# Linear attention on one core: K and V loaded with 8 KB from each row, KV products made by two halves of the array

## The chip, the cores and the metric

The kernel runs on one core of a Trainium2 chip. The metric is the device time of one execution in microseconds (us); lower is better.

## The reference

Q, K and V are float32 of shape 8 x 12 x 512 x 64: 96 heads of 512 rows with 64 columns.

```python
Q_feat = np.maximum(0, Q)
K_feat = np.maximum(0, K)
KV = np.einsum('bhkd,bhkv->bhdv', K_feat, V)
K_sum = np.sum(K_feat, axis=2)
numerator = np.einsum('bhqd,bhdv->bhqv', Q_feat, KV)
denominator = np.einsum('bhqd,bhd->bhq', Q_feat, K_sum)
return (numerator / (denominator[:, :, :, None] + 1e-10)).astype(np.float32)
```

There is no softmax: per head a 64 x 64 matrix KV and a vector of sums are made from K and V, and each row of Q is multiplied by them.

## The kernel before

The 96 heads are worked in twelve octets of eight heads (NO = 12), one octet in a step. An array X in DRAM is read as a flat row of numbers that is cut into blocks of 128 partitions (`view`).

**Loads.** Q of an octet is one block: each partition gets 8 KB of float32, which is 32 rows of a head, so a head lies on 16 partitions. K and V are cut into blocks of half an octet (g, four heads): each partition gets 4 KB, 16 rows, and a head lies on 32 partitions. For most octets (o < PAIRS = 9) the two blocks of K come in one transfer of two pieces of 4 KB for each partition (line 181), likewise V; the last three octets load each half by itself (line 187). These transfers are issued by POOL and turn float32 into bfloat16 on the way. Octet 0's K and V are loaded in float32 by SP in four transfers into two output buffers (line 277). POOL issues in the order K, V, Q of octets 1 to 7, and then a store of an octet before each further octet's loads; its transfers use ten semaphores in turn (LANES), so each issue waits until the transfer ten before it has landed. Stores of octets 0 to 3 go by POOL (line 262), the others by SP (line 265), where they wait for the first half of the last octet's K; the last octet's store is cut in two.

**The products of a step.** A matmul contracts over partitions, and four heads share the 128 partitions of a block, so heads are kept apart by masks of zeros. DVE's `prep_k` (line 201) writes K's positive part twice, in the columns s = 0 and 1, times `mask[:, 0, s]`, which keeps every second head. `prep_v` (lines 210 and 212, one of four by ACT) writes V twice, in t = 0 and 1, times `mask[:, 1, t]`. One matmul of 128 weight columns (two s by 64) and 132 moving columns (two t by 66) then yields four heads at once; the extra columns of ones give K_sum. Sixteen of them, one for each row of a partition, make up a half octet g, accumulated in `ps_kv[:, g]` (line 397); both halves' sums lie in one PSUM bank. `evac_kv` (line 227, four copies by ACT) brings the sums to `kvd`.

On PE a step is a loop body: transposes of q2 into ps_qt (line 390), the KV products (397), transposes of the octet before, ot, into ps_x (406), the denominators ps_den (384), and the numerators ps_x (384). DVE turns ps_den into reciprocals (`own`, `den`, `rec`, lines 240 to 247) and divides (`norm`, line 252) into the output buffer.

The order on each engine is written out by hand in `step`; the class `Order` adds the semaphore waits from what each operation reads and writes. PE's loop waits for named semaphores: q2, then a0 and d0 (masked K and V of the first half) and d1 (of the second), t0 and t1, qt and ev, n0 and n1. In `setup`, DVE writes the masks by memsets, prepares octet 0, and derives `mask_h`, which later picks each partition's own head out of the denominators, from a 128 x 128 identity that POOL makes. Two `prep_k` stand for each half octet, and `copy_q` (216) hands a landed Q to PE.

Of the kernel before, what the change touches and what calls it, by code (L numbers as in the profile page):

```python
# [89 lines left out]
def kernel(  # L90
# [8 lines left out]
    B, H, S, D = Q.shape  # L99
    assert D == 64  # L100
    P = 128
    D1 = D + 1
    D4 = D + 4
    NH = B * H
    R = S * 4 // P
    RQ = S * 8 // P
# [17 lines left out]
    def view(X, f):  # L124
        return X.rearrange("b h s d -> (b h s d)").rearrange("(n p f) -> n p f", p=P, f=f)

    Qr, Kr, Vr, Or = view(Q, RQ * D), view(K, R * D), view(V, R * D), view(out, RQ * D)

    ident = sb.tile([P, P], bf16, name="ident")
    ident32 = sb.tile([P, P], fp32, name="ident32")  # L130
# [13 lines left out]
    k_sb = [sb.tile([P, 2, R * D], bf16, name=f"k_sb{i}") for i in range(NI)]  # L144
    v_sb = [sb.tile([P, 2, R * D], bf16, name=f"v_sb{i}") for i in range(NI)]
    o_sb = [sb.tile([P, RQ, D], fp32, name=f"o_sb{i}") for i in range(NOUT)]
    ps_kv = psum.tile([P, 2, 256], fp32, name="ps_kv")
    ps_den = psum.tile([P, 2, 256], fp32, name="ps_den")
    ps_qt = [psum.tile([P, U // 2, P], bf16, name=f"ps_qt{j}") for j in range(2)]
    ps_x = [psum.tile([P, 1024], fp32, name=f"ps_x{j}") for j in range(2)]  # L150

    names = ["dve", "act", "pool", "pe", "q2", "a0", "d0", "d1", "qt", "ev", "t0", "t1", "n0", "n1"]
    lanes = {"pool": [f"gl{i}" for i in range(LANES)], "sp": [f"sl{i}" for i in range(4)],
             "last": [f"el{i}" for i in range(5)]}
    sems = {n: tc.alloc_semaphore("s_" + n) for n in names + sum(lanes.values(), [])}
# [2 lines left out]
    def lane(who):  # L158
        turn[who] += 1
        return lanes[who][(turn[who] - 1) % len(lanes[who])]  # L160
# [1 line left out]
    do = Order(nc, sems)  # L162

    def kv_src(g):
        if g < 2:
            kv = o_sb[g].rearrange("p (c r) d -> p c r d", c=2)
            return kv[:, 0], ("o", g, 0), kv[:, 1], ("o", g, 1)
        i, j = (g // 2) % NI, g % 2
        r = [x[i][:, j].rearrange("p (r d) -> p r d", d=D) for x in (k_sb, v_sb)]
        return r[0], ("k", i, j), r[1], ("v", i, j)  # L170

    def load_q(o):
        do.op("pool", lambda e: e.dma_start(out=q_sb[o % NI].rearrange("p u f -> p (u f)"), in_=Qr[o],  # L173
# [3 lines left out]
    def load_kv(o, halves=(0, 1)):  # L177
        i = o % NI
        if o < PAIRS:
            for n, X, t in (("K", Kr, k_sb), ("V", Vr, v_sb)):  # L180
                do.op("pool", lambda e: e.dma_start(out=t[i], in_=X[2 * o:2 * o + 2].rearrange("g p f -> p g f"),  # L181
                                                    single_packet=True),
                      writes=[(n.lower(), i, 0), (n.lower(), i, 1)], dma=lane("pool"))
            return
        for j in halves:
            for n, X, t in (("K", Kr, k_sb), ("V", Vr, v_sb)):
                do.op("pool", lambda e: e.dma_start(out=t[i][:, j], in_=X[2 * o + j], single_packet=True),  # L187
                      writes=[(n.lower(), i, j)], dma=lane("pool"))

    def load(o):  # L190
# [45 lines left out]
              reads=[("x", j)], writes=[("ot", j)], sem=f"t{j}")  # L236

    def denominators():
        ps = ps_den[:, 0].rearrange("p (u h c) -> p u (h c)", u=U, h=8)
        do.op("dve", lambda e: e.scalar_tensor_tensor(  # L240
            own.rearrange("p u h c -> p u (h c)"), ps, 1e-10,
            mask_h.rearrange("p h c -> p (h c)").unsqueeze(1).to_broadcast([P, U, 16]), op0=Alu.add, op1=Alu.mult),
            reads=["pd", "mask_h"], writes=["own"])
        do.op("dve", lambda e: e.tensor_reduce(  # L244
            out=den.rearrange("p (u c) -> p u c", c=2), in_=own.rearrange("p u h c -> p u c h"), op=Alu.add,
            axis=mybir.AxisListType.X), reads=["own"], writes=["den"])
        do.op("dve", lambda e: e.reciprocal(rec, den), reads=["den"], writes=["rec"])  # L247
# [17 lines left out]
            do.op("sp", lambda e: e.dma_start(out=to, in_=src), reads=keys, dma=lane("sp" if o < NO - 4 else "last"))  # L265

    KF = [[("kf", g, 0), ("kf", g, 1), ("vo", g, 0), ("vo", g, 1), ("vo1", g)] for g in range(2)]
    QT = [("qt", 0), ("qt", 1)]
    OT = [("ot", 0), ("ot", 1)]

    def memset(who, ap, value, key):
        do.op(who, lambda e: e.memset(ap, value), writes=[key] if isinstance(key, (str, tuple)) else key)

    def body():
        for g in range(2):
            for n, X, j in (("k", Kr, 0), ("v", Vr, 1)):
                do.op("sp", lambda e: e.dma_start(
                    out=o_sb[g].rearrange("p (c r) d -> p c (r d)", c=2)[:, j], in_=X[g]),
                    writes=[("o", g, j)], dma=lane("sp"))
        load_q(0)  # L280
        memset("pool", ident, 0.0, "ident")
        do.op("pool", lambda e: e.affine_select(out=ident, in_=ident, compare_op=Alu.not_equal, fill=1.0, base=0,
                                                pattern=[[-1, P]], channel_multiplier=1),
              reads=["ident"], writes=["ident"])
        for o in range(1, AHEAD + 1):
            load(o)
            if o == 1:
                setup()
        for o in range(NO + 1):
            step(o)  # L290
        nc.gpsimd.drain()
        for n in lanes["pool"] + lanes["sp"]:
            nc.gpsimd.wait_ge(sems[n], do.count[n])

    def setup():
        for h in range(4):
            for s in range(2):
                memset("dve", mask[32 * h:32 * h + 32, 0, s:s + 1], 1.0 if h % 2 == s else 0.0, ("m", h, s))
        for t in range(2):
            memset("dve", mask[:, 1, t:t + 1], 0.0, ("m", 4, t))  # L300
        for t in range(2):
            do.op("dve", lambda e: e.memset(mask[64 * t:64 * t + 64, 1, t:t + 1], 1.0), writes=[("m", 4, t), "mask"])
        for g in range(2):
            ones = vo[g][:, :, :, 1:D4 - 1]
            memset("dve", ones[:, :, :, 0:D + 2:D1], 0.0, ("vo1", g))
            for t in range(2):
                memset("dve", ones[64 * t:64 * t + 64, :, t, 0:D + 2:D1], 1.0, ("vo1", g))
        prep_k(0, 0)
        prep_k(0, 1)
        prep_v(0, 0, "dve", "d0")  # L310
        prep_v(0, 1, "act", "a0")
        do.op("dve", lambda e: e.tensor_copy(ident32, ident), reads=["ident"], writes=["ident32"])
        for c in range(2):
            do.op("dve", lambda e: e.tensor_reduce(
                out=mask_h[:, :, c], in_=ident32.rearrange("p (h b) -> p h b", h=8), op=Alu.add,
                axis=mybir.AxisListType.X), reads=["ident32"], writes=[("mh", c), "mask_h"])
        do.op("dve", lambda e: e.memset(kvf.bitcast(fp32)[:, 0:4 * D1], 0.0), writes=KVD, sem="n0")
        do.op("dve", lambda e: e.memset(kvf.bitcast(fp32)[:, 4 * D1:], 0.0), writes=KVD, sem="n1")
        copy_q(0)
        prep_k(1, 0)  # L320
        prep_k(1, 1)
        prep_v(1, 0, "dve")
        prep_v(1, 1, "dve", "d1")
        for j in range(2):
            nc.scalar.sem_inc(sems[f"t{j}"], 1)
            do.note("act", "act", (), (), f"t{j}", 1)

    def step(i):
# [15 lines left out]
        if not last:  # L344
            do.looped([("q2", r)], ["q2", "ident"], [("pq", 0)])
            do.looped([], ["q2", "ident"], [("pq", 1)])
            relu_q(0)
            relu_q(1)
            do.looped([("a0", r), ("d0", r)], KF[0], [("pk", 0)])
            do.looped([("d1", r)], KF[1], [("pk", 1)])  # L350
            evac_kv()
            if more and not late:
                prep_v(2 * i + 2, 1, "act", "a0")
                first()
# [25 lines left out]
    def products():  # L380
        pe = nc.tensor

        def mm(out_, lhsT, rhs):
            return pe.matmul(out_, lhsT, rhs, start=True, stop=True, skip_group_check=True)  # L384

        with pe.Fori(1, NO + 2, 1) as r:
            with pe.If(r < NO + 1):
                pe.wait_ge(sems["q2"], r)
                for u in range(U):
                    x = pe.transpose(ps_qt[u // 8][:, u % 8, :], q2[:, u, :], ident)  # L390
                    if u % 8 == 7:
                        x.then_inc(sems["pe"], 1)
                for g in range(2):
                    for s in ("a0", "d0") if g == 0 else ("d1",):
                        pe.wait_ge(sems[s], r)
                    for k in range(R):
                        x = pe.matmul(  # L397
                            ps_kv[:, g, 0:2 * (D + 2)].rearrange("p (t d) -> p t d", t=2),
                            kf[g][:, k, :, :].rearrange("p s d -> p (s d)"), vo[g][:, k, :, 1:D4 - 1],
                            start=(k == 0), stop=(k == R - 1), skip_group_check=True)  # L400
                    x.then_inc(sems["pe"], 1)
            with pe.If(r > 1):
                pe.wait_ge(sems["t0"], r)
# [6 lines left out]
            with pe.If(r < NO + 1):  # L410
                pe.wait_ge(sems["qt"], r)
                pe.wait_ge(sems["ev"], r)
                for u in range(U):
                    x = mm(ps_den[:, 0].rearrange("p (u h) -> p u h", u=U)[:, u], qt[:, u, :],
                           kvd[:, :, 0:2 * D1:2 * D1 - 1])
                x.then_inc(sems["pe"], 1)
                q = qt.rearrange("p u (h c) -> p u h c", h=8)
# [47 lines left out]
```

## Time and profile before

| what | before |
|---|---|
| median of 3 runs | 126.06 us (125.84 to 127.11) |
| the profiled execution | 125.83 us, of which the span is 124.1 |
| busy in the span | PE 87.2 us, DVE 87.5, ACT 78.4, POOL 29.6 |
| granted TensorE clock, mean | 0.903 |
| moved | 37.75 MB read from HBM, 12.58 MB written |

Times in the profile are microseconds from the start of the span. A row of the groups gives line, engine, operation, the tile written and the tiles read, shapes, the number of instructions, their busy time and mean duration in ns, and the idle time of the engine just before them with what ended it. PE is the matmuls, PEld the weight loads, which overlap them. A row of the timeline gives start, length, engine, line and operation; the square brackets hold the idle time before it and what ended that. In the page's slices each figure stands for a fortieth of the span, in tenths; PEclk is the granted clock of TensorE.

### The profile page before, as it was taken

To read this page: it belongs to the slowest core of one execution; us is meant where nothing else is said; L and a number is where in the kernel's file an instruction comes from. 1 tells how busy PE (TensorE), PEld (TensorE's weight loads), DVE (VectorE), ACT (ScalarE), POOL (GpSimd) and SP (SyncE) were. 2 spreads that over 40 slices of the span, in tenths; PEclk is the share of its full clock that TensorE was granted. 3 is DMA by queue.
4 is the path that set the end of the run, shared out by engine and by line. 5 is a ranking of instruction groups with operands and counts; after the bars stand their busy time and mean duration, and the time that the engine had idled before them with its cause. 6 is when DMAs were issued, how large, how long until landed. Compare 5 with 4: busy or idle time off the path is not lost.

```text
span 124.1 us, 2677 instructions
## 1 busy us (share of the span) xinstructions
PE 87.2 (70%) x1056; PEld 75.6 (61%) x1056; DVE 87.5 (71%) x180; ACT 78.4 (63%) x108; POOL 29.6 (24%) x50
## 2 busy tenths in 40 slices
PE   0007849755998989989796973998936996794600
PEld 0007739642995969879594961896923993592500
DVE  2746409369679999989979549799289319939530
ACT  0253299362949999999897980989953945953000
POOL 5992214122431442113111323151200000000000
PEclk9999995995589999999999997699995589999995
DMA  3999999999999999999999999999999999999993
GB/s 118 328 273 284 214 208 211 215 208 215 209 213 211 211 215 209 214 211 211 217 377 199 215 363 229 209 331 260 213 282 310 216 293 348 431 431 425 431 408 128
DMA packets 10260, 32.54 MB, mean 262 GB/s; under 512 B 912, under 2 KB 912, under 8 KB 8848
## 3 DMA queue, kind: packets, MB, share of 16 engines
q0 software_dynamic: 8384, 22.02, 83.1%
q1 hardware_dynamic: 1872, 10.49, 20.7%
q14 instruction: 4, 0.03, 0.1%
HBM read 37.75 MB, written 12.58 MB: 406 GB/s over the span
## 4 chain that ended last, share of the span: by engine, by line
DMA 66%; DVE 14%; PE 8%; issue 4%; POOL 3%; POOLq 0%; DVEq 0%; SPq 0%
DMA q_sb<-in_Q_dram 34%; DMA v_sb<-in_V_dram 20%; DMA k_sb<-in_K_dram 13%; DVE o_sb L252 8%; PE ps_kv L397 3%; PE ps_x L406 2%; DVE kf L201 2%; PE ps_qt L390 1%; DVE vo L212 1%; POOL q_sb L173 1%; POOL v_sb L181 1%; DVE ot_sb L235 1%; PE ps_x L384 1%; DVE den L244 1%; DVE rec L247 1%
## 5 line engine op out<-in xcount | busy, mean ns | idle before, releaser
L252 DVE TENSOR_TENSOR o_sb<-ps_x,rec 128x1024 f32<-128x1024 f32 x24 | 28.2, 1217 | 8.2 <-PE ps_x L406 7.9
L235 ACT COPY ot_sb<-ps_x 128x1024 f32<-128x1024 f32 x23 | 23.2, 1012 | 15.3 <-PE ps_x L384 13.8
L397 PE MATMUL ps_kv<-vo,kf 128*128 128x132 bf16 x384 | 28.9, 239 | 1.8 <-DVE vo L212 1.8
L397 PEld LDWEIGHTS ps_kv<-vo,kf 128*128 128x128 bf16 x384 | 26.9, 107 | 2.6 <-DVE vo L212 2.3
L384 PE MATMUL ps_x<-qt,kvd 128*128 128x256 bf16 x96 | 17.5, 316 | 13.5 <-DVE o_sb L252 13.1
L219 ACT ACTIVATE qt<-ps_qt 128x1024 bf16<-128x1024 bf16 x24 | 23.3, 1029 | 3.3 <-PE ps_qt L390 3.3
L227 ACT CAST kvd<-ps_kv 64x260 bf16<-64x260 f32 x48 | 18.0, 374 | 10.9 <-PE ps_kv L397 9.6
L390 PE MATMUL ps_qt<-ident,q 128*128 128x128 bf16 x192 | 16.6, 255 | 11.2 <-DVE q L216 11.2
L406 PE MATMUL ps_x<-ident,ot_sb 128*128 128x128 f32 x192 | 23.0, 273 | 1.7 <-DVE ot_sb L235 1.7
L390 PEld LDWEIGHTS ps_qt<-ident,q 128*128 128x128 bf16 x192 | 14.6, 117 | 13.7 <-DVE q L216 11.8
L406 PEld LDWEIGHTS ps_x<-ident,ot_sb 128*128 128x128 f32 x192 | 20.8, 141 | 2.0 <-issue 2.0
L216 DVE COPY q<-q_sb 128x2048 bf16<-128x2048 bf16 x12 | 8.2, 687 | 17.1 <-DMA q_sb<-in_Q_dram 16.1
L384 PEld LDWEIGHTS ps_x<-qt,kvd 128*128 128x128 bf16 x96 | 8.5, 108 | 19.0 <-DVE o_sb L252 17.7
L201 DVE TENSOR_SCALAR kf<-k_sb,mask 128x1024 bf16<-128x1024 bf16 x44 | 19.5, 467 | 0.6 <-PE ps_kv L397 0.6
L212 DVE TENSOR_SCALAR vo<-v_sb,mask 128x1024 bf16<-128x1024 bf16 x33 | 14.9, 481 | 0.0
L210 ACT ACTIVATE vo<-v_sb,mask 128x1024 bf16<-128x1024 bf16 x11 | 12.7, 1153 | 0.3
L173 POOL DMA_DIRECT2D q_sb<-in_Q_dram x12 | 7.5, 623 | 14.7 <-DMA v_sb<-in_V_dram 8.1
L384 PEld LDWEIGHTS ps_den<-kvd,qt 128*128 128x128 bf16 x192 | 6.0, 96 | 4.2 <-issue 4.2
L181 POOL DMA_DIRECT2D v_sb<-in_V_dram x8 | 5.8, 727 | 10.1 <-DMA k_sb<-in_K_dram 8.3
L384 PE MATMUL ps_den<-kvd,qt 128*128 128x16 bf16 x192 | 6.9, 179 | 1.8 <-ACT kvd L227 1.8
L181 POOL DMA_DIRECT2D k_sb<-in_K_dram x8 | 6.0, 751 | 7.5 <-DMA q_sb<-in_Q_dram 6.3
L187 POOL DMA_DIRECT2D k_sb<-in_K_dram x6 | 3.3, 544 | 11.7 <-DMA out_dram<-o_sb 4.2
(23 smaller groups left out, 32.8 us busy)
## 6 DMA issues: line engine op xcount, KB each, us to landing
out_dram<-o_sb SPq DMA_DIRECT2D x7, 1024.0 KB, 12.4
q_sb<-in_Q_dram POOLq DMA_DIRECT2D x12, 512.0 KB, 23.2
k_sb<-in_K_dram POOLq DMA_DIRECT2D x8, 512.0 KB, 24.6
v_sb<-in_V_dram POOLq DMA_DIRECT2D x8, 512.0 KB, 24.6
out_dram<-o_sb POOLq DMA_DIRECT2D x4, 1024.0 KB, 22.2
k_sb<-in_K_dram POOLq DMA_DIRECT2D x6, 256.0 KB, 17.9
v_sb<-in_V_dram POOLq DMA_DIRECT2D x6, 256.0 KB, 18.4
o_sb<-in_K_dram SPq DMA_DIRECT2D x2, 512.0 KB, 5.7
```

Source lines behind the costliest of these rows:

```text
L181: do.op("pool", lambda e: e.dma_start(out=t[i], in_=X[2 * o:2 * o + 2].rearrange("g p f -> p g f"), single_packet=True), writes=[(n.lower( ...
L201: do.op("dve", lambda e: e.tensor_scalar(kf[g % 2][:, :, s, :], src, scalar1=0.0, scalar2=mask[:, 0, s:s + 1], op0=Alu.max, op1=Alu.mult), ...
L210: make = lambda e: e.activation(to, src, Act.Copy, scale=m)
L212: make = lambda e: e.tensor_scalar(to, src, scalar1=m, scalar2=None, op0=Alu.mult)
L219: do.op("act", lambda e: e.activation(qt[:, j * (U // 2):(j + 1) * (U // 2)], ps_qt[j], Act.Relu), reads=[("pq", j)], writes=[("qt", j)], ...
L227: do.op("act", lambda e: e.copy(kvd[64 * c:64 * c + 64, s:8:2, c * D1:c * D1 + D1].rearrange("p (g t) d -> p g t d", t=2), ps_kv[64 * s:64 ...
L235: do.op(who, lambda e: e.copy(to, src) if who == "act" else e.tensor_copy(to, src), reads=[("x", j)], writes=[("ot", j)], sem=f"t{j}")
L252: do.op("dve", lambda e: e.tensor_tensor(o_sb[i][:, rs], ps_x[j].rearrange("p (r d) -> p r d", d=D), rec[:, rs].unsqueeze(2).to_broadcast( ...
L384: return pe.matmul(out_, lhsT, rhs, start=True, stop=True, skip_group_check=True)
L390: x = pe.transpose(ps_qt[u // 8][:, u % 8, :], q2[:, u, :], ident)
L397: x = pe.matmul(ps_kv[:, g, 0:2 * (D + 2)].rearrange("p (t d) -> p t d", t=2), kf[g][:, k, :, :].rearrange("p s d -> p (s d)"), vo[g][:, k ...
L406: x = pe.transpose(ps_x[u // 8][:, u % 8 * P:u % 8 * P + P], ot[:, u].rearrange("p h c -> p (h c)"), ident32)
```

## The change

K and V are cut as Q is: 8 KB for each partition, 32 rows of a head, a head on 16 partitions, eight heads on the 128. The transfers of a whole octet have one piece of 8 KB for each partition; those of half an octet (octet 0 and the last three) now take half of each 8 KB. So g is no longer four of the heads, but half of the rows of all eight.

The two masks together keep one head of four, which now leaves two of the eight. So each KV matmul is made twice, on partitions 0 to 63 and on 64 to 127, as matmuls of 64 rows by 128 columns. Each half of the array has its own sums in its own PSUM bank, over both g: 32 matmuls for each half where there were 16 for each g, so 64 in a step in place of 32. `ps_kv` takes two banks, and `ps_den` moves into the upper part of its second one. Therefore PE waits, ahead of the KV products, for a new semaphore dn, which `own` raises after reading ps_den. `mask[:, 0]` changes every 16 partitions and is computed from mask_h, which moves ahead of octet 0's preparation with ident32; the `vo` columns of ones are set by four memsets of 32 partitions in place of two of 64.

```diff
-    Qr, Kr, Vr, Or = view(Q, RQ * D), view(K, R * D), view(V, R * D), view(out, RQ * D)
+    Qr, Kr, Vr, Or = [view(X, RQ * D) for X in (Q, K, V, out)]
...
-    ps_kv = psum.tile([P, 2, 256], fp32, name="ps_kv")
-    ps_den = psum.tile([P, 2, 256], fp32, name="ps_den")
+    ps_kv = psum.tile([P, 2, 512], fp32, name="ps_kv")
+    ps_den = ps_kv[:, 1, 256:512]
...
-                do.op("pool", lambda e: e.dma_start(out=t[i], in_=X[2 * o:2 * o + 2].rearrange("g p f -> p g f"),
+                do.op("pool", lambda e: e.dma_start(out=t[i].rearrange("p j f -> p (j f)"), in_=X[o],
...
-                do.op("pool", lambda e: e.dma_start(out=t[i][:, j], in_=X[2 * o + j], single_packet=True),
+                do.op("pool", lambda e: e.dma_start(out=t[i][:, j], in_=X[o][:, R * D * j:R * D * (j + 1)],
+                                                    single_packet=True),
...
-            reads=["pd", "mask_h"], writes=["own"])
+            reads=["pd", "mask_h"], writes=["own"], sem="dn")
...
         for h in range(4):
-            for s in range(2):
-                memset("dve", mask[32 * h:32 * h + 32, 0, s:s + 1], 1.0 if h % 2 == s else 0.0, ("m", h, s))
-        for t in range(2):
-            memset("dve", mask[:, 1, t:t + 1], 0.0, ("m", 4, t))
-        for t in range(2):
-            do.op("dve", lambda e: e.memset(mask[64 * t:64 * t + 64, 1, t:t + 1], 1.0), writes=[("m", 4, t), "mask"])
+            for t in range(2):
+                do.op("dve", lambda e: e.memset(mask[32 * h:32 * h + 32, 1, t:t + 1], 1.0 if h % 2 == t else 0.0),
+                      writes=[("m", h, t), "mask"])
         for g in range(2):
             ones = vo[g][:, :, :, 1:D4 - 1]
             memset("dve", ones[:, :, :, 0:D + 2:D1], 0.0, ("vo1", g))
-            for t in range(2):
-                memset("dve", ones[64 * t:64 * t + 64, :, t, 0:D + 2:D1], 1.0, ("vo1", g))
+            for h in range(4):
+                memset("dve", ones[32 * h:32 * h + 32, :, h % 2, 0:D + 2:D1], 1.0, ("vo1", g))
+        do.op("dve", lambda e: e.tensor_copy(ident32, ident), reads=["ident"], writes=["ident32"],
+              sem="dn")
+        for c in range(2):
...
+        do.op("dve", lambda e: e.tensor_reduce(
+            out=mask[:, 0, :], in_=mask_h[:, :, 0].rearrange("p (a s) -> p s a", s=2), op=Alu.add,
+            axis=mybir.AxisListType.X), reads=["mask_h"], writes=["mask"])
         prep_k(0, 0)
...
-                    for s in ("a0", "d0") if g == 0 else ("d1",):
+                    for s in ("dn", "a0", "d0") if g == 0 else ("d1",):
                         pe.wait_ge(sems[s], r)
                     for k in range(R):
-                        x = pe.matmul(
-                            ps_kv[:, g, 0:2 * (D + 2)].rearrange("p (t d) -> p t d", t=2),
-                            kf[g][:, k, :, :].rearrange("p s d -> p (s d)"), vo[g][:, k, :, 1:D4 - 1],
-                            start=(k == 0), stop=(k == R - 1), skip_group_check=True)
+                        for h in range(2):
+                            ps = slice(64 * h, 64 * h + 64)
+                            x = pe.matmul(
+                                ps_kv[:, h, 0:2 * (D + 2)].rearrange("p (t d) -> p t d", t=2),
+                                kf[g][ps, k, :, :].rearrange("p s d -> p (s d)"), vo[g][ps, k, :, 1:D4 - 1],
+                                start=(g + k == 0), stop=(g == 1 and k == R - 1), skip_group_check=True)
```

More of the change, by code (lines that the diff above doesn't have):

```diff
@@ L146 @@
     o_sb = [sb.tile([P, RQ, D], fp32, name=f"o_sb{i}") for i in range(NOUT)]
-    ps_kv = psum.tile([P, 2, 256], fp32, name="ps_kv")
-    ps_den = psum.tile([P, 2, 256], fp32, name="ps_den")
+    ps_kv = psum.tile([P, 2, 512], fp32, name="ps_kv")
+    ps_den = ps_kv[:, 1, 256:512]
     ps_qt = [psum.tile([P, U // 2, P], bf16, name=f"ps_qt{j}") for j in range(2)]
     ps_x = [psum.tile([P, 1024], fp32, name=f"ps_x{j}") for j in range(2)]
-    names = ["dve", "act", "pool", "pe", "q2", "a0", "d0", "d1", "qt", "ev", "t0", "t1", "n0", "n1"]
+    names = ["dve", "act", "pool", "pe", "q2", "a0", "d0", "d1", "dn", "qt", "ev", "t0", "t1", "n0", "n1"]
     lanes = {"pool": [f"gl{i}" for i in range(LANES)], "sp": [f"sl{i}" for i in range(4)],
@@ L164, in kv_src @@
     def kv_src(g):
[L165 to L170, printed above, removed]
+        o, j = g // 2, g % 2
+        kv = (o_sb[0], o_sb[1]) if o == 0 else [x[o % NI].rearrange("p j (r d) -> p (j r) d", d=D) for x in (k_sb, v_sb)]
+        key = [("o", c, j) if o == 0 else (c, o % NI, j) for c in ((0, 1) if o == 0 else "kv")]
+        return kv[0][:, R * j:R * j + R], key[0], kv[1][:, R * j:R * j + R], key[1]
     def load_q(o):
@@ L238, in denominators @@
     def denominators():
-        ps = ps_den[:, 0].rearrange("p (u h c) -> p u (h c)", u=U, h=8)
+        ps = ps_den.rearrange("p (u h c) -> p u (h c)", u=U, h=8)
         do.op("dve", lambda e: e.scalar_tensor_tensor(
@@ L267 @@
     KF = [[("kf", g, 0), ("kf", g, 1), ("vo", g, 0), ("vo", g, 1), ("vo1", g)] for g in range(2)]
+    PK = [("pk", 0), ("pk", 1)]
     QT = [("qt", 0), ("qt", 1)]
@@ L274, in body @@
     def body():
-        for g in range(2):
-            for n, X, j in (("k", Kr, 0), ("v", Vr, 1)):
+        for j in range(2):
+            for c, X in enumerate((Kr, Vr)):
                 do.op("sp", lambda e: e.dma_start(
-                    out=o_sb[g].rearrange("p (c r) d -> p c (r d)", c=2)[:, j], in_=X[g]),
-                    writes=[("o", g, j)], dma=lane("sp"))
+                    out=o_sb[c][:, R * j:R * j + R].rearrange("p r d -> p (r d)"),
+                    in_=X[0][:, R * D * j:R * D * (j + 1)]), writes=[("o", c, j)], dma=lane("sp"))
         load_q(0)
@@ L305, in setup @@
             memset("dve", ones[:, :, :, 0:D + 2:D1], 0.0, ("vo1", g))
-            for t in range(2):
-                memset("dve", ones[64 * t:64 * t + 64, :, t, 0:D + 2:D1], 1.0, ("vo1", g))
+            for h in range(4):
[4 more added lines that the diff above has]
+            do.op("dve", lambda e: e.tensor_reduce(
+                out=mask_h[:, :, c], in_=ident32.rearrange("p (h b) -> p h b", h=8), op=Alu.add,
+                axis=mybir.AxisListType.X), reads=["ident32"], writes=[("mh", c), "mask_h"])
+        do.op("dve", lambda e: e.tensor_reduce(
+            out=mask[:, 0, :], in_=mask_h[:, :, 0].rearrange("p (a s) -> p s a", s=2), op=Alu.add,
+            axis=mybir.AxisListType.X), reads=["mask_h"], writes=["mask"])
         prep_k(0, 0)
@@ L311, in setup @@
         prep_v(0, 1, "act", "a0")
[L312 to L316, printed above, removed]
         do.op("dve", lambda e: e.memset(kvf.bitcast(fp32)[:, 0:4 * D1], 0.0), writes=KVD, sem="n0")
@@ L348, in step @@
             relu_q(1)
-            do.looped([("a0", r), ("d0", r)], KF[0], [("pk", 0)])
-            do.looped([("d1", r)], KF[1], [("pk", 1)])
+            do.looped([("dn", r), ("a0", r), ("d0", r)], KF[0], PK + ["pd"])
+            do.looped([("d1", r)], KF[1], PK + ["pd"])
             evac_kv()
@@ L413, in products @@
                 for u in range(U):
-                    x = mm(ps_den[:, 0].rearrange("p (u h) -> p u h", u=U)[:, u], qt[:, u, :],
+                    x = mm(ps_den.rearrange("p (u h) -> p u h", u=U)[:, u], qt[:, u, :],
                            kvd[:, :, 0:2 * D1:2 * D1 - 1])
```

## The prediction

> **What bounds the kernel now.** The page's slices come first, then its DMA queues: is anything busy from end to end?
>
> ```profile
> PEclk9999995995589999999999997699995589999995
> DMA  3999999999999999999999999999999999999993
> GB/s 118 328 273 284 214 208 211 215 208 215 209 213 211 211 215 209 214 211 211 217 377 199 215 363 229 209 331 260 213 282 310 216 293 348 431 431 425 431 408 128
> ...
> q0 software_dynamic: 8384, 22.02, 83.1%
> q1 hardware_dynamic: 1872, 10.49, 20.7%
> ```
>
> The DMA row is full in 38 of 40 slices. GB/s counts bytes written: a load that turns f32 into bf16 reads twice what it writes, so 211 in the middle is about 422 read, close to the 431 of the plain f32 stores at the end. The two queues together hold 103.8% of sixteen engines' span: packets overlap a little on an engine, so a packet's duration is not its cost. The spacing of transfers is. I read it from POOL's timeline, where each issue waits until the transfer ten before it has landed:
>
> ```profile
> 21.05 0.71 POOL L181 DMA_DIRECT2D v_sb<-in_V_dram  x1 [1.77 <-DMA k_sb<-in_K_dram]
> 23.49 0.56 POOL L173 DMA_DIRECT2D q_sb<-in_Q_dram  x1 [1.73 <-DMA v_sb<-in_V_dram]
> 25.94 0.70 POOL L181 DMA_DIRECT2D k_sb<-in_K_dram  x1 [1.90 <-DMA q_sb<-in_Q_dram]
> 28.49 0.71 POOL L181 DMA_DIRECT2D v_sb<-in_V_dram  x1 [1.85 <-DMA k_sb<-in_K_dram]
> 30.96 0.56 POOL L173 DMA_DIRECT2D q_sb<-in_Q_dram  x1 [1.75 <-DMA v_sb<-in_V_dram]
> ```
>
> An issue released by a K landing and the next one, released by V, differ by V's transfer: 2.44 us; then Q 2.45, K 2.55, V 2.47. A step of the loop takes three such transfers, 7.4 us. How much of that does the compute need? The timeline of one step in the middle:
>
> ```profile
> 61.73 2.06 PE L397 MATMUL ps_kv<-vo,kf 128*128 128x132 bf16 x32
> ...
> 63.08 0.69 DVE L216 COPY q<-q_sb 128x2048 bf16<-128x2048 bf16 x1 [0.62 <-DMA q_sb<-in_Q_dram]
> ...
> 63.62 1.91 PE L406 MATMUL ps_x<-ident,ot_sb 128*128 128x128 f32 x16
> ...
> 65.28 2.34 DVE L252 TENSOR_TENSOR o_sb<-ps_x,rec 128x1024 f32<-128x1024 f32 x2
> ```
>
> DVE is idle 0.62 us, waiting for Q's landing, so it needs about 6.8 of the 7.4 us. PE's loop is as long: from the division at 65.28 (2.34) over the ps_x products (0.61), the transposes (1.06), the KV products (2.06) to the first half of the L406 transposes (0.95), the blocks' recorded ends overlapping a little, the next division could start at about 72.05, 6.77 us later. Loads pace the steps; compute follows with some 0.65 us to spare. Last, the chain of what ended last, its end:
>
> ```profile
> 73.28 17.10 DMA q_sb<-in_Q_dram
> ...
> 97.82 3.00 PE ps_kv L397 x32
> ...
> 108.63 1.12 PE ps_kv L397 x16
> ...
> 116.52 2.36 DVE o_sb L252 x2
> ```
>
> The last wait on a load ends at 90.38; then 28.5 us of compute lead to 118.88, where the last half store can start. In the trace's landing records the last stores land every 2.45 us, the two halves at 121.7 and 122.95: they leave the queue without a gap. An unhindered half-MB transfer takes about 3.2 us (the first SP load, issued at 0.95, landed at 4.17), so the compute would allow an end at 122.1. The end is set by the transfers, and compute has about 0.8 us to spare there.
>
> **The change, part by part.**
>
> *K and V rows of 8 KB.* Sixteen transfers (K and V of octets 1 to 8) now have 128 packets instead of 256; octet 0 and octets 9 to 11 are still moved as 4 KB from each row. Q already has the new shape: 8 KB read, 4 KB written. So Q against K/V prices the edit. By durations (packet records of the trace): 173.7 ns for a K/V packet, 324.5 for a Q packet; 2 x 173.7 - 324.5 = 22.9 ns, times 2,048 pairs, over 16 engines: 2.9 us saved. That is the upper end, since durations overlap. By spacing: eighteen issue intervals from 18.57 to 63.28 average 2.51 us for K/V and 2.43 for Q; without one disturbed neighbouring pair (2.82 and 2.31), 2.48 and 2.45. Times 16: 1.3 or 0.5 us. A fit of packet starts over the steady stretch (155 ns for a K/V packet, about 303 for a Q packet) gives 7 ns x 2,048 / 16 = 0.9. The lower end is nothing. I take 0.7 us, between the spacings, which are nearest to what the queue does. As the transfers run to the end without a gap, 0.7 us earlier at octet 8 is 0.7 us earlier at the last store, and the last Q that compute waits for lands that much earlier too.
>
> *KV products by halves.* Each step's 32 pairs of weight load and matmul become 64 pairs of 64 rows, alternating between the halves, in two PSUM banks. No row of before shows matmuls of two halves side by side. The bounds:
>
> ```profile
> L397 PE MATMUL ps_kv<-vo,kf 128*128 128x132 bf16 x384 | 28.9, 239 | 1.8 <-DVE vo L212 1.8
> L397 PEld LDWEIGHTS ps_kv<-vo,kf 128*128 128x128 bf16 x384 | 26.9, 107 | 2.6 <-DVE vo L212 2.3 <-ACT vo L210 0.3
> ...
> L384 PE MATMUL ps_den<-kvd,qt 128*128 128x16 bf16 x192 | 6.9, 179 | 1.8 <-ACT kvd L227 1.8
> ```
>
> In the middle 32 pairs take 2.06 us, 64 ns each. One after another, 64 pairs take 4.1 us: +2.06 a step. If halves overlap wholly, what is left is issue: the ps_den block runs 16 pairs with only 16 moving columns in 0.58 us, 36 ns a pair, so 64 take 2.3 us: +0.25. A gain below 2.06 is excluded, since every pair still has a 128-column weight load and must be issued. I take +0.4, near the overlapping end, because the halves share neither rows nor PSUM bank. That is 7.2 us of PE loop against 7.4 us of loads, so it hides in the middle. Without the cover it would be 0.4 us times the steps. In the tail two KV blocks are on the path; of the second only the half after d1 is. That is 1.5 x 0.4 = 0.6 us, inside the 0.8 us to spare.
>
> On this the Trainium skill speaks both ways. "TensorEngine Tiling (Array Packing)", section "Key Properties", says that different tiles can execute weight loads and matmuls in parallel, which is the overlapping end; it also says that changing the tiling mode drains the engine, and each step changes it twice. "TensorE: Matmul & The Clock Gate", section "Single matmul latency", gives (398 + N)/2.4 ns warm; as an estimate two such drains at N = 132 are 0.44 us a step, by which the tail would grow by about 0.7 us more and the forecast rise to about 126.
>
> *ps_den in the second KV bank.* PE must now wait (dn) until own of the step before has read the denominators, ahead of its first KV matmul; queued behind are that block and all PE work after it. At 60.11 to 60.52 own is over before the KV block begins at 61.73, behind the ps_x products and transposes; in the tail own ends at 104.4 and KV begins at 107.1. Cost nothing; without the 1.06 us of transposes as cover, some 0.3 us a step. ACT's four ps_kv copies keep their form (64x260, 374 ns).
>
> *Setup.* The eight mask memsets and four more ones memsets are chained, at about 0.17 us wait each (as the vo memsets show); ident32, the two mask_h reductions (0.29 each) and a third now precede the first kf. Some 1 + 1 + 2 us later: the first kf goes from 4.20 to about 7.4, the first q copy from 9.35 to about 10.1. V's second half, landing at 12.7, then releases DVE as before; step 1's copy waits 4.15 us for Q in any case. PE would begin step 1 at most 0.3 us later, and it idles 0.76 us there. Cost nothing; uncovered, 0.3 us once. POOL and SP have as many issues in the same order.
>
> The sum against the profiled execution (125.83 us: span 124.1, 1.7 around it) is -0.7, 125.1; against the median of 126.06 it is **125.4 us**.
>
> **Rivals.**
>
> *The halves run one after another* (the change doesn't do what it says for PE). The KV block takes 4.1 us, the PE loop 6.77 + 2.06 = 8.83, more than the loads' 7.4, so PE becomes the pace. Step 1 starts at 18.3; nine steps on is 97.8 instead of 90.5. The tail grows from 28.5 to about 30 us (the KV blocks cost 0.9 and 1.4 more, the transposes, no longer after an idle stretch at the half clock of slices 30 and 31, 0.85 less). 127.8 and 3.2 us of store give 131 against 122.95: about 134 us. For it: consecutive weight loads of L397 are already 60 ns apart. Against: separate rows and banks. It decides from about +1.1 us a block: then the tail's 1.5 x 1.1 uses up the 0.8 to spare and the 0.7 gained; at +1.3, step 10 starts 0.8 us late and the end is near 128.
>
> *Packet durations are the cost.* Then all 2.9 us are gained in transfers: 123.2, if the compute tail, starting as much earlier, is at most 0.8 longer. Against: 103.8%, and Q's landings hardly closer than K's.
>
> *The rows don't matter at all*: 2.48 against 2.45 is chance, and PE stays hidden: 126.0, no change.
>
> **How the numbers follow.** Forecast 0.49 (own range 124.6 to 126.2); rows without effect 0.17; packet durations, wholly or half, 0.14; halves mostly or wholly serial 0.20, of which half lies above 129. Faster by over 1% (below 124.8, about what a measurement can tell here) are the third case and a little of the first: 0.20. Slower by over 1% is the serial case and some of its border: 0.24. The rest, 0.56, is within 1%. Range 123.9 to 129.0: one in ten above it, less than one in ten below.
>
> **What would show it.** Right: PE ps_kv blocks of 2.2 to 2.6 us in the middle, DVE's q copy still released by Q's landing each step, K/V issue intervals of 2.44 to 2.46, about 2,048 packets fewer in q0, a DMA row full to the end. Wrong: KV blocks near 4 us with DVE's division waiting for L406 in each step; intervals near 2.3 (durations were the cost) or unchanged; gaps between the last stores' landings, which would mean that the tail's compute sets the end.

## The result and the profile after

The changed kernel takes 130.33 us (median of 4, 130.05 to 134.69; the 134.69 ran at a mean granted clock of 0.71 and is not in the ratio). The kernel before took 126.05 beside it. The ratio is 1.0315 (95% interval 1.0242 to 1.0388); a second measurement on another chip gave 130.09 and 1.0342 (1.0309 to 1.0375). The forecast was 125.4 us with a range of 123.9 to 129.0. It was wrong in size and in sign.

The profiled execution has a span of 128.5 us, 4.4 more than before. First the groups, where the serial rival had placed the danger:

```profile
L400 PE MATMUL ps_kv<-vo,kf 64*128 64x132 bf16 x768 | 27.5, 230 | 2.1 <-DVE vo L211 2.1
...
L400 PEld LDWEIGHTS ps_kv<-vo,kf 64*128 64x128 bf16 x768 | 24.9, 100 | 4.0 <-DVE vo L211 2.3
```

There are twice as many matmuls, 768, and their busy time is 27.5 us, where 384 took 28.9. In the block the two halves overlap wholly. One step of the timeline shows it with its neighbours:

```profile
42.28 1.06 PE L391 MATMUL ps_qt<-ident,q 128*128 128x128 bf16 x16
...
43.28 2.07 PE L400 MATMUL ps_kv<-vo,kf 64*128 64x132 bf16 x64
...
45.27 1.97 PE L409 MATMUL ps_x<-ident,ot_sb 128*128 128x128 f32 x16
...
46.40 1.22 DVE L251 TENSOR_TENSOR o_sb<-ps_x,rec 128x1024 f32<-128x1024 f32 x1 [0.29 <-PE ps_x L409]
```

64 pairs take 2.07 us; 32 took 2.06. PE lost nothing in the block, so the transfers come next. The page's slices and queues:

```profile
DMA  3999999999999999999999999999999999999753
GB/s 94 233 269 273 249 214 214 214 213 212 214 213 214 212 214 213 213 217 212 282 307 209 258 322 152 223 339 232 206 328 251 209 338 422 415 423 416 321 237 138
...
q0 software_dynamic: 6336, 22.02, 78.8%
q1 hardware_dynamic: 1872, 10.49, 20.8%
q14 instruction: 4, 0.03, 0.1%
q8 instruction: 1, 0.02, 0.0%
```

The 2,048 packets are gone from q0, and the middle runs at 212 to 217. But slices 1 to 3, counted from 0, moved 233, 269 and 273 where they moved 328, 273 and 284, and the last three 321, 237 and 138 where they moved 431, 408 and 128. The end is no longer full: the DMA row falls to 7, 5, 3. And a row is new: one packet in a queue q8 of instructions. POOL's timeline shows where the transfers fall behind (each issue follows the landing of the transfer ten before it, named in the bracket):

```profile
23.66 0.69 POOL L179 DMA_DIRECT2D v_sb<-in_V_dram  x1 [2.77 <-DMA k_sb<-in_K_dram]
25.80 0.53 POOL L171 DMA_DIRECT2D q_sb<-in_Q_dram  x1 [1.46 <-DMA v_sb<-in_V_dram]
...
77.55 0.53 POOL L185 DMA_DIRECT2D k_sb<-in_K_dram  x1 [1.88 <-DMA out_dram<-o_sb]
80.47 0.53 POOL L185 DMA_DIRECT2D v_sb<-in_V_dram  x1 [2.40 <-DMA k_sb<-in_K_dram]
```

In the first pair K of octet 2 releases V's issue at 23.66; before, the same issue (K of octet 2 landed) came at 21.05. In the last pair the landing of octet 9's first half of K, half the size of a whole transfer, came 2.92 us after the store's; before, the same interval was 77.04 - 75.98 = 1.06:

```profile
75.98 0.53 POOL L187 DMA_DIRECT2D k_sb<-in_K_dram  x1 [2.08 <-DMA out_dram<-o_sb]
77.04 0.53 POOL L187 DMA_DIRECT2D v_sb<-in_V_dram  x1 [0.53 <-DMA k_sb<-in_K_dram]
```

A transfer is over when the last of its sixteen engines is. The landing records give all sixteen, so the distance from the first engine to the last is a measure of how far some engines are behind:

| first to last engine, us | Q of octet 2 | first K half of octet 9 | store of octet 10 |
|---|---|---|---|
| before | 0.49 | 0.80 | 1.11 |
| after | 1.85 | 3.58 | 4.08 |

From Q of octet 2 to the last load of a whole octet, landings 28 to 75 us after the start, this distance stays between 1.8 and 1.9 us: what is behind does not catch up. The records do not name the engines, so that it is the same one each time is inferred. At the store of octet 9 the first engine is done at 117.78, 0.9 us later than before (116.87), the last at 122.40, 4.4 later (117.99). From there the last engine's landings follow each other about as they did before, to the end, so these 4.4 us are the loss. The loss builds up in two places, the start and the loads of octets 9 to 11, and there stand the half-octet loads: 4 KB out of every 8 KB, where they had read one contiguous block. In the packet records, of the 512 packets of SP's four loads of octet 0, 34 took over 198 ns before (median 172) and 144 after.

### The profile page after: what moved, and what is told of

Same layout as the page of the kernel before. It is cut to its first block, busy times and chain, and to the rows that moved or that the text cites. A ratio compares the mean times of both kernels' runs of the same rounds, so it can differ in the third digit from the quotient of the medians.

```text
span 128.5 us, 3447 instructions
## 1 busy us (share of the span) xinstructions
PE 89.1 (69%) x1440; PEld 75.9 (59%) x1440; DVE 88.0 (68%) x181; ACT 78.3 (61%) x108; POOL 27.4 (21%) x50
## 4 chain that ended last, share of the span: by engine, by line
DMA 82%; DVE 5%; PE 4%; issue 3%; POOL 2%; POOLq 0%; SPq 0%
DMA out_dram<-o_sb 35%; DMA v_sb<-in_V_dram 27%; DMA q_sb<-in_Q_dram 19%; PE ps_x L409 3%; DVE o_sb L251 3%; PE ps_kv L400 1%; DVE ot_sb L234 1%; DVE vo L211 1%; POOL q_sb L171 0%; POOL k_sb L185 0%; POOL k_sb L179 0%; DVE den L243 0%; DVE rec L246 0%; DVE own L239 0%; POOL ident L282 0%
## 5 line engine op out<-in xcount | busy, mean ns | idle before, releaser
L400 PE MATMUL ps_kv<-vo,kf 64*128 64x132 bf16 x768 | 27.5, 230 | 2.1 <-DVE vo L211 2.1
L400 PEld LDWEIGHTS ps_kv<-vo,kf 64*128 64x128 bf16 x768 | 24.9, 100 | 4.0 <-DVE vo L211 2.3
L409 PE MATMUL ps_x<-ident,ot_sb 128*128 128x128 f32 x192 | 24.9, 286 | 1.7 <-DVE ot_sb L234 1.7
L391 PE MATMUL ps_qt<-ident,q 128*128 128x128 bf16 x192 | 16.0, 249 | 13.2 <-DVE q L215 13.2
L409 PEld LDWEIGHTS ps_x<-ident,ot_sb 128*128 128x128 f32 x192 | 22.1, 147 | 3.2 <-issue 2.0
L385 PE MATMUL ps_kv<-kvd,qt 128*128 128x16 bf16 x192 | 6.9, 179 | 1.8 <-ACT kvd L226 1.8
L385 PEld LDWEIGHTS ps_kv<-kvd,qt 128*128 128x128 bf16 x192 | 6.0, 97 | 2.7 <-issue 2.0
L179 POOL DMA_DIRECT2D k_sb<-in_K_dram x8 | 5.1, 641 | 11.5 <-DMA q_sb<-in_Q_dram 9.6
L179 POOL DMA_DIRECT2D v_sb<-in_V_dram x8 | 4.8, 606 | 11.4 <-DMA k_sb<-in_K_dram 9.7
L185 POOL DMA_DIRECT2D v_sb<-in_V_dram x6 | 4.1, 675 | 10.0 <-DMA k_sb<-in_K_dram 4.2
```

Of the source, the lines that this page charges most:

```text
L179: do.op("pool", lambda e: e.dma_start(out=t[i].rearrange("p j f -> p (j f)"), in_=X[o], single_packet=True), writes=[(n.lower(), i, 0), (n ...
L400: x = pe.matmul(ps_kv[:, h, 0:2 * (D + 2)].rearrange("p (t d) -> p t d", t=2), kf[g][ps, k, :, :].rearrange("p s d -> p (s d)"), vo[g][ps, ...
L409: x = pe.transpose(ps_x[u // 8][:, u % 8 * P:u % 8 * P + P], ot[:, u].rearrange("p h c -> p (h c)"), ident32)
```

## The experiments

Two theories. **A**: the half-octet loads with their 8 KB pitch have slow packets, which leave some engines behind. **B**: the delay comes with the 64-row products or with PE's longer program. Times are medians; ratios are against the kernel before on the same chip.

**e1_contig**: half loads from contiguous blocks again.

```diff
-                do.op("pool", lambda e: e.dma_start(out=t[i][:, j], in_=X[o][:, R * D * j:R * D * (j + 1)],
+                do.op("pool", lambda e: e.dma_start(out=t[i][:, j], in_=half[id(X)][2 * o + j],
...
-                    in_=X[0][:, R * D * j:R * D * (j + 1)]), writes=[("o", c, j)], dma=lane("sp"))
+                    in_=half[id(X)][j]), writes=[("o", c, j)], dma=lane("sp"))
```

> The changed kernel, but the half-octet loads of K and V (octets 0, 9, 10, 11) read one contiguous block of 128 x 4 KB, as before the change, instead of 4 KB out of every 8 KB; destinations, order and sizes stay. (The rows of these octets are then mixed over the heads, so this part of the products is changed.) Theory A, the 8 KB pitch of these loads slows their packets and leaves some DMA engines behind: the 2 us at the start and the growth of the gap between first and last engine in octets 9 to 11 vanish, 125.0 to 125.6 us. Theory B, the delay comes with the 64-row products or the larger program: nothing changes, 130 us.

126.65 us, ratio 1.0030 (1.0006 to 1.0054). Some 3.5 us of the loss are gone. The slow packets on SP's loads fall from 144 to 12, those of the late halves of octets 9 to 11 from 33 to none. Theory A holds for the bulk, but 126.65 is above the 125.6 that it expected.

**e2_before_strided**: the pitch alone, put into the kernel before.

```diff
-                do.op("pool", lambda e: e.dma_start(out=t[i][:, j], in_=X[2 * o + j], single_packet=True),
+                do.op("pool", lambda e: e.dma_start(out=t[i][:, j], in_=row[id(X)][o][:, R * D * j:R * D * (j + 1)],
+                                                    single_packet=True),
...
-                    out=o_sb[g].rearrange("p (c r) d -> p c (r d)", c=2)[:, j], in_=X[g]),
+                    out=o_sb[g].rearrange("p (c r) d -> p c (r d)", c=2)[:, j], in_=row[id(X)][0][:, R * D * g:R * D * (g + 1)]),
```

> The kernel before, with one part of the change alone: its half-octet loads of K and V (octets 0, 9, 10, 11) read 4 KB out of every 8 KB. (The heads of these octets are mixed, that part of the products is changed.) Theory A: the whole loss appears here without 64-row products and without 8 KB rows, 130 to 131.5 us. Theory B: 126 us as before.

130.23 us, ratio 1.0321 (1.0281 to 1.0362): as slow as the changed kernel, with the old products and the old whole loads. 161 of SP's 512 packets are slow, and the last store of octet 10 has 3.28 us from its first engine to its last. Theory A is shown from both sides.

**e3_old_loads**: the changed kernel with all loads of K and V as before; against e1 it has in addition

```diff
-                do.op("pool", lambda e: e.dma_start(out=t[i].rearrange("p j f -> p (j f)"), in_=X[o],
+                do.op("pool", lambda e: e.dma_start(out=t[i], in_=half[id(X)][2 * o:2 * o + 2].rearrange("g p f -> p g f"),
```

> The changed kernel with every load of K and V as before the change (two blocks of 128 x 4 KB in a transfer, halves contiguous), so with the 64-row products, the moved ps_den and the new setup alone. (Heads are mixed, so the products' values are changed.) Theory A: the products cost nothing, 125.8 to 126.4 us, and the distance to e1_contig is what the 8 KB rows of octets 1 to 8 bring: 0.5 to 1.0 us. Theory B: about 130 us.

126.76 us, ratio 1.0048 (1.0016 to 1.0079). Two things follow. The 8 KB rows of octets 1 to 8 bring 126.76 - 126.65 = 0.1 us, less than the 0.5 expected and within the spread of the runs. And the change without any of its loads is still 0.7 us slower than before, which theory A does not explain. Its trace has the q8 row of the changed kernel, and so have e1 and e4; e2 and the kernel before do not. It is one packet of 16 KB that lasts 944 ns and starts 18 to 23 us after the start (21.3 in the changed kernel), about when PE's loop jumps back for the first time; at the landings that follow, one engine is about 1 us further behind. That became a theory of its own, **P**: PE's longer loop body needs one more load of instructions.

**e5_padded**: the kernel before, with only its PE loop body made longer.

```diff
+            with pe.If(r > NO):
+                for k in range(32):
+                    pe.matmul(ps_kv[:, 0, 0:2 * (D + 2)].rearrange("p (t d) -> p t d", t=2),
+                              kf[0][:, k % R, :, :].rearrange("p s d -> p (s d)"), vo[0][:, k % R, :, 1:D4 - 1],
+                              start=True, stop=True, skip_group_check=True)
```

> The kernel before, with 32 more pairs of weight load and matmul in PE's loop body, run only in the last pass, after PE's last useful product, so that the body is as long as the changed one's. Theory P, the longer body makes one more load of instructions (the 16 KB packet of queue 8, 944 ns, seen once in every run with the 64-row products and in none without), which puts one DMA engine about 0.9 us behind for the rest: the packet appears and the time is 126.5 to 126.9 us. Theory S, the 0.7 us of e3_old_loads over before come from the new setup or the wait for dn: no change, 126.0.

126.63 us, ratio 1.0038 (1.0011 to 1.0066), within what theory P expected, and the packet is there, in the DMA view of this run:

```profile
q0 software_dynamic: 8384, 22.02, 82.3%
...
q8 instruction: 1, 0.02, 0.0%
```

The packet starts at 20.59 us. At the landing of 20.68 the last engine was 0.03 us behind the second last; at the next, 24.17, it is 1.03 behind, and it stays near 1 us at the transfers that follow. The last half of V lands at 109.11, where it landed at 107.25 before, and the compute of the last octet waits for it. So a longer body of PE's loop is paid for on a DMA engine: 0.6 us here, for 944 ns of one engine of sixteen. Of e3's 0.7 us that leaves 0.1, within the spread, for the new setup and the wait for dn.

**e4_zigzag**: the halves are cut so that neither takes only even or only odd pieces of 4 KB.

```diff
+    def part(X, o, j):
+        x = X[o].rearrange("(a b) (c f) -> a (b c) f", b=2, f=R * D)
+        return x[:, 1:3] if j else x[:, 0:4:3]
...
-                do.op("pool", lambda e: e.dma_start(out=t[i][:, j], in_=X[o][:, R * D * j:R * D * (j + 1)],
+                do.op("pool", lambda e: e.dma_start(out=t[i][:, j], in_=part(X, o, j),
```

> The changed kernel, but the first half loads 4 KB at offsets 0 and 12 KB of every 16 KB and the second those at 4 and 8 KB, for K and V alike: the sums over rows are the same, each packet is still 4 KB, but a transfer no longer takes only even or only odd 4 KB pieces. Theory A1, the regular 8 KB pitch loads only part of the memory at a time: about as fast as e1_contig, 125.0 to 126. Theory A2, any reading with holes is slow: 129 to 131. Theory B: 130.

126.95 us, ratio 1.0056 (1.0028 to 1.0084). Theory A1's side: 0.3 us over e1. It is 1 us above its range, which, like that of e1, had not counted what theory P is about. Only 25 of SP's packets are slow. Reading 4 KB pieces with holes is not slow as such.

**e8_pitch12** and **e11_pitch16**: 4 KB out of every 12 KB, and out of every 16 KB.

```diff
+    def pitch(X, o, j):
+        flat = X.rearrange("n p f -> (n p f)")
+        at = max(0, o - 6) * 3 * 128 * 1024 // 1 + 1024 * j
+        return flat[at:at + 128 * 3 * 1024].rearrange("(p f) -> p f", f=3 * 1024)[:, 0:1024]
```

(The other likewise, with 4 in place of 3; its octets begin elsewhere in the arrays.)

> The changed kernel, but its half loads read 4 KB out of every 12 KB. (The rows of octets 0, 9, 10 and 11 are others, that part of the products is changed.) If the regular 8 KB pitch is what is slow, because it takes only every second piece of 4 KB, then a pitch of 12 KB, which takes odd and even pieces in turn, is as fast as the zigzag: 126.5 to 127.2 us. If holes in the read as such are slow, 129.5 to 131.

> The changed kernel, but its half loads read 4 KB out of every 16 KB. (The rows of octets 0, 9, 10 and 11 are others, that part of the products is changed.) If what is slow is that only pieces of one parity of 4 KB are read at a time, 16 KB does the same as 8 KB or worse: 130 us or more. If it is something peculiar to the halves of an 8 KB row, 16 KB is as good as 12 KB: 127 us.

127.00 us, 1.0061 (1.0029 to 1.0093), with 25 slow packets on SP's loads; and 130.87 us, 1.0397 (1.0347 to 1.0446), with 120. So the pitches of 8 and 16 KB, where all pieces have the same parity of 4 KB, are slow, and 12 KB, where it alternates, is not. It is the number of slow packets that differs, not the slowest one: what they took beyond 172 ns is together 20.0 us in the changed kernel and in e11, 7.1 in e8, 7.0 in e4 and 2.9 before, though single packets of e8 reached 1,099 ns. What in the memory does this is not shown by these runs, nor is how other pitches do, nor why the slow packets hit some engines more than others.

**e6_zig_tail**: the zigzag in octets 9 to 11 alone (the POOL line of e4's diff).

> The changed kernel with the zigzag of e4 in octets 9 to 11 alone; octet 0 keeps the 8 KB pitch. If octet 0 and the tail each have their part of the loss, as the landings of the changed kernel show (2 us late after the start, nearly 3 more in octets 9 to 11): 128 to 129 us. If the loss is octet 0's alone, 130; if the tail's alone, 127.

127.91 us, ratio 1.0138 (1.0094 to 1.0182), just under the range expected for a part in each place. By ratios, octet 0's pitch costs 1.0138 - 1.0056 = 0.8%, 1.0 us, and the tail's 1.0342 - 1.0138 = 2.0%, 2.6 us. The later one costs more, though fewer of its packets are slow; its slow ones are longer, the longest 1,311 ns where SP's reached 789; that this is the reason is not shown.

**e7_zig_first**: e4 with an empty first pass of PE's loop, so that the packet comes early.

```diff
-        with pe.Fori(1, NO + 2, 1) as r:
+        with pe.Fori(0, NO + 2, 1) as r:
+          with pe.If(r > 0):
```

> e4_zigzag with one empty pass of PE's loop ahead of the first, so that the loop's first jump back comes about 1 us after the start, when the DMA engines have little to do. Theory P: the 16 KB packet comes early and costs nothing, 126.1 to 126.5 us, or, where it comes only with the first full pass, stays where it is, 126.9. Theory S: 126.9.

127.11 us, ratio 1.0076 (1.0041 to 1.0111): no gain, though the packet did move to 2.4 us after the start (1,133 ns long). The engines already have loads queued there. The distance of first to last engine is smaller for a long while (0.80 at Q of octet 2, e4 has 1.47), but then the halves of octets 9 to 11 bring it to 2.27 at the store of octet 10, e4's being 2.05. The experiment does not tell P and S apart; e5 had done so.

**e9_whole**: no half loads at all.

```diff
-    PAIRS = NO - 3
+    PAIRS = NO
...
+        for c, X in enumerate((Kr, Vr)):
+            do.op("sp", lambda e: e.dma_start(out=o_sb[c].rearrange("p r d -> p (r d)"), in_=X[0]),
+                  writes=[("o", c, 0), ("o", c, 1)], dma=lane("sp"))
...
-            if o < NO - 1:
+            if o < 2:
                 store(o)
             if o + AHEAD + 1 < NO:
                 load(o + AHEAD + 1)
+            if 2 <= o < NO - 1:
+                store(o)
```

> The changed kernel without any half-octet load: octets 0 and 9 to 11 come by whole rows of 8 KB too, in the order K, V, Q, and the stores of octets 2 and 3 stand behind the loads of 10 and 11. If holes were all that the change lost beyond the 16 KB packet of instructions, it ends at 126.0 to 126.6 us: the packet costs 0.6, the 8 KB rows bring about 0.4, and the tail's compute may start up to one transfer later. If whole loads let the tail's compute set the end: 127 to 128.

125.91 us, ratio 1.0004 (0.9974 to 1.0033), just under the range expected: 4 us better than the change, and the same as the kernel before. The DMA row of its page is full almost to the end again, and the q8 packet is still there:

```profile
DMA  3999999999999999999999999999999999999974
...
q8 instruction: 1, 0.02, 0.0%
```

**e10_short**: e9 with every second KV product left out, so that the body has 32 pairs again.

```diff
-                    for k in range(R):
+                    for k in range(0, R, 2):
                         for h in range(2):
...
-                                start=(g + k == 0), stop=(g == 1 and k == R - 1), skip_group_check=True)
+                                start=(g + k == 0), stop=(g == 1 and k == R - 2), skip_group_check=True)
```

> e9_whole with every second of the KV products left out (k = 0, 2, ..., 14 only, so half of each sum is missing), 32 pairs in PE's body as before the change. Theory P: the 16 KB packet of queue 8 is gone and the time is 0.5 to 0.9 us under e9_whole. If PE's products themselves cost something beyond the packet, the difference is larger than 1 us; if neither, it is nothing.

125.52 us, ratio 0.9967 (0.9953 to 0.9982). The packet is gone from the DMA view:

```profile
q0 software_dynamic: 5472, 22.02, 80.0%
q1 hardware_dynamic: 1584, 10.49, 20.7%
q14 instruction: 4, 0.03, 0.1%
```

The gain over e9 is 0.4 us, a little less than expected. It can't be put down to the packet alone: in e9's trace the chain of what ended last holds no wait on a transfer after 63.38 us, only compute, and e10 has half the products in that stretch. That the packet comes and goes with the length of the body is shown; what it costs is shown by e5. e10 is also what is left of the change's intention: with all rows of 8 KB and no extra packet the time is 0.3% below the kernel before, but this kernel makes only half the products. A complete version with so short a body was not tried.

**after_again**: the changed kernel on e9's chip.

> The changed kernel once more, on the chip of this call, for the comparison with e9_whole and e10_short: 130 to 130.5 us by either theory.

130.09 us.

## Why the prediction was wrong

**The step that failed** is the sentence on the loads that were thought unchanged: octet 0 and octets 9 to 11 "are still moved as 4 KB from each row". Their packets have the same size as before, and I costed them at nothing. But the rows had become 8 KB, so the same 4 KB now come at a pitch of 8 KB instead of one after another. That term is 3.4 to 4.2 us (130.09 - 126.65; 130.23 - 126.03), nearly the whole loss of 4.1 to 4.3. It made some engines late, and the slowest of them set the end. None of the rivals held it: they asked what the new shape would do, and not what the change had done to the address pattern of the shape that stayed. The price list could not hold it either, since every load in the trace of before read one contiguous stretch for each block; that absence was the thing to bound.

**A second term was missing**: PE's longer loop body. It was priced by PE's issue rate alone, and the load of its instructions was not thought of. It costs 0.6 us by e5. The compute's margin in the tail was read too small, which would have spoken for the forecast: in e5 the last half store, with all engines done within 0.18 us of each other, lands 2.6 us after its issue (121.41 to 124.02), not 3.2. By that the compute had about 1.4 us to spare before the change, not 0.8.

**The 8 KB rows** were put at 0.7 us. The 18 intervals between POOL's issues from 30.74 to 75.05 average 2.462 us; before, the same 18, from 28.49 to 73.28, average 2.488. Eleven of the eighteen end at a landing of K or V, so that is (44.79 - 44.31) / 11 = 0.04 us each, and 0.7 for sixteen, as forecast. Yet the times of e3 and e1 differ by 0.1 only. The interval is shortened as predicted; what of it reaches the end, these runs do not settle. The rival of packet durations (2.9 us) is out in any case.

**The products** hid under the loads as forecast, with other terms. The block costs 0.01 us more, not 0.4; it even runs below the 2.3 us that the prediction took as the least for 64 pairs (32 ns a pair, where ps_den's 36 was the bound). But the hand-overs around it grew. The transposes ahead of it started 2.79 us before the L406 block (60.83 to 63.62); now it is 42.28 to 45.27, 2.99. The step, from one KV block to the next where compute ran unhindered (43.28, 50.40, 57.51 in the timeline after), is 7.12 us, where I had predicted 7.2 from 6.77. The base was too low: where the kernel before ran unhindered, its KV blocks start at 40.85, 47.75 and 54.62, 6.9 us apart. So the change costs a step 0.2 to 0.3 us, not 0.4, and the nearness of 7.2 is partly luck. The serial rival is excluded. The Trainium skill ("TensorEngine Tiling (Array Packing)", "Key Properties") states that a change of tiling mode drains the engine. Two changes a step and hand-overs that are longer by 0.1 us on either side of the block would fit that, but no run here tells it from other causes; the prediction's estimate of 0.44 us for two drains was twice the 0.2 measured.

**The dn wait and the setup** cost nothing clear of the noise, as said (0.1 us between e3 and e5). The first kf came at 5.74, not at 7.4; the first Q copy came at 11.31, not at 10.1: it waited 2.32 us for Q, which landed at 11.29; with contiguous halves, in e1, Q landed at 9.02.

**The sum, put right**: 126.0 + 3.4 (pitch) + 0.6 (instructions) - 0.1 (8 KB rows) = 129.9, against 130.1 to 130.3 measured. This is close by construction, since the 3.4 is itself the difference between the changed kernel and e1; with e2's independent 4.2 it is 130.7.

## What to carry to other kernels

When a layout changes, list every transfer that touches it and write down its address pattern, those too whose packet size stays the same: here 4 KB pieces at a pitch of 8 or 16 KB were slow, contiguous, at a pitch of 12 KB or in the zigzag they were not. Where the transfers run without a gap to the end, the slowest of sixteen engines sets the time, so look at the distance from first to last engine and not only at the mean rate. And a loop body that grows may cost on the DMA side too.

## What the runs showed of the hardware that was not expected

- Loads of 4 KB pieces at a pitch of 8 or 16 KB had 144 and 120 of 512 packets slower than 198 ns (median 172), 20.0 us beyond the median in all; at 12 KB or in the zigzag it was 25, and 7.1 or 7.0 us; contiguous, in the kernel before, 34 and 2.9 us. The Trainium skill ("DMA: Bandwidth & Descriptors", "Latency and other measured facts") reports slow copies between HBM tensors at row pitches that are large powers of two, from 2 MiB up. Here slow packets are seen at 8 KB already, the pieces being 4 KB; whether the cause is the same, no run here shows.
- Two halves of the array, each with its own PSUM bank, overlapped wholly: 64 pairs of 64 rows took 2.07 us, 32 of 128 rows 2.06.
- A PE loop body of 120 pairs of weight load and matmul brought one 16 KB packet of instructions, 944 ns on one DMA engine, about when it first jumped back; bodies of 88 pairs did not.
